# The end of a decoder trunk on one core: the last accumulation in two column groups, its squares in three parts, its update in three pieces

## The chip, the core and the metric

The kernel runs on one core of a Trainium2 chip, in one launch. The metric is the device time of an execution in microseconds. Five engines work side by side, each through its own queue of instructions: TensorE (PE, with its weight loads shown as PEld), VectorE (DVE), ScalarE (ACT), GpSimd (POOL) and SyncE (SP). SP, ACT and POOL also issue transfers.

## The reference

A decoder trunk of two layers on 256 tokens of 1024 columns in float32. The first layer mixes tokens by a gated linear recurrence, the second by attention with a forget gate. In each layer a half-step feed-forward block stands before and after the mixer. What matters here is the very last step, the second feed-forward block of the second layer:

```python
def rms_norm(x, g):
    xf = x.astype(jnp.float32)
    y = xf * lax.rsqrt(jnp.mean(xf * xf, axis=-1, keepdims=True) + EPS)
    return (y * g.astype(jnp.float32)).astype(x.dtype)

def swiglu(x, w_gate, w_up, w_down):
    return (jax.nn.silu(x @ w_gate) * (x @ w_up)) @ w_down
...
        f = swiglu(rms_norm(h, ffn2_pre_g[layer]), ffn2_w_gate[layer], ffn2_w_up[layer], ffn2_w_down[layer])
        h = h + 0.5 * rms_norm(f, ffn2_post_g[layer])
    return h
```

`w_down` is 2816 x 1024. The last norm needs the sum of squares over all 1024 columns of a token before any column of the output can be finished.

## The kernel before, in words

The 256 tokens are two halves of 128 (t = 0 and t = 1), which lie on the 128 partitions. `h[0]` and `h[1]` hold the residual stream, 128 x 1024 each. Every matrix is worked through in items of up to 1024 columns of weights: an item is loaded into a `raw` tile, split into an upper and a lower part (`whi` by ACT, `wlo` by DVE), and multiplied with both halves of the tokens. A product of full precision is made of three on TensorE (`mm3`): upper by upper, upper by lower part of the weights, lower part of the tokens by upper part of the weights. The input of the last matrix is the hidden layer, in `hhi` and `hlo`.

The order of TensorE's instructions is that in which the program is written (a manual schedule); the other engines' instructions are placed by a scheduler, with those under `tc.high_priority()` ahead. Half 0 leads and half 1 follows some items behind.

The last matrix `w_down` has 22 items of 128 rows (`row_items`). Each half has two accumulators of 128 x 512 in PSUM, `acc[t][0]` and `acc[t][1]`, of four `mm` tiles in all. For the last feed-forward block the last four items are kept for half 1 (`rows` = 4): they are first all multiplied into the first accumulator and then all into the second, so that the first is complete 12 products of 512 columns before the second:

```python
                    todo = [(kk, uu, n) for n in range(2) for (kk, uu) in kept[t]]
```

Then `post(t, acc[t])` calls `enter`, here with `last=True`. It does these steps for the half:

- `square_sum` on ACT, one for each accumulator: the squares go to a `junk` tile that nobody reads, their sum into a column of `ss`. One `junk` tile serves all.
- `rstd_of`: sum of the two columns plus epsilon (on DVE, tile `nv`), then the power -1/2 on POOL (`rstd`).
- the multiply of each accumulator by the gain `gb` on DVE, into a tile `t1` (512 columns each).
- `scalar_tensor_tensor` on DVE in pieces: `h` = `t1` times `rstd` plus `h`, and a transfer to `out` behind each piece. Half 0 has pieces of 256, 256 and 512 columns, all on SP's queue; half 1 has four of 256, on SP's and ACT's queues in turn.

In the profile the pages' names leave buffer numbers out; `mm_8053` and `mm_8054` in the rows of the order are the two accumulators of half 1, `mm_7982` and `mm_7983` those of half 0, `h_72` and `h_73` the halves of the stream.

Of the kernel before, what the change touches and what calls it, by code (L numbers as in the profile page):

```python
# [9 lines left out]
F32 = mybir.dt.float32  # L10
# [3 lines left out]
ALU = mybir.AluOpType  # L14
AX = mybir.AxisListType

P = 128
D = 1024
# [9 lines left out]
EPS = 1e-6  # L28
# [16 lines left out]
def trunk_kernel(ctx: ExitStack, tc: tile.TileContext, A: dict, out: bass.AP):  # L45
    nc = tc.nc
# [6 lines left out]
    spool = ctx.enter_context(tc.tile_pool(name="small", bufs=4))  # L53
# [4 lines left out]
    def nm(s):  # L58
        uid[0] += 1
        return f"{s}_{uid[0]}"  # L60

    def mmbank():
        return psum.tile([P, 512], F32, tag="mm", name=nm("mm"), bufs=4)

    def gtbank():
        return psum.tile([P, 512], F32, tag="gt", name=nm("gt"), bufs=2)
# [7 lines left out]
    def tensor_work(n):  # L74
        pace["t"] += n * 0.445e-3
# [5 lines left out]
    def defer(n, fn):  # L81
        pend.append([n, fn])
# [23 lines left out]
    h = [hpool.tile([P, D], F32, tag=f"h{t}", name=f"h{t}") for t in range(2)]  # L106
# [9 lines left out]
    mhalf = cpool.tile([P, 1], F32, name="mhalf")  # L116
# [48 lines left out]
    def split(rawv, parts, n, pieces=1, pin=False):  # L165
        u = Unit()
        hi = wpool.tile([P, 1024], F32R, tag="whi", name=nm("whi"), bufs=WB)
        lo = wpool.tile([P, 1024], F32R, tag="wlo", name=nm("wlo"), bufs=WB)
        m = n // pieces
        for c in range(0, n, m):  # L170
            up = nc.scalar.activation(hi[:parts, c:c + m], rawv[:, c:c + m], AF.Copy)  # L171
            if settled[0] or pin:
                tc.keep_in_program_order(up)
                settled[0] = False
            nc.vector.tensor_tensor(lo[:parts, c:c + m], rawv[:, c:c + m], hi[:parts, c:c + m].bitcast(F32), ALU.subtract)  # L175
        u.hi, u.lo = hi[:parts, :n], lo[:parts, :n]
        return u

    def mm3(ps, xh, xl, wh, wl, first, last):
        tensor_work(3 * wh.shape[1])  # L180
        nc.tensor.matmul(ps, xh, wh, start=first, stop=False)  # L181
        nc.tensor.matmul(ps, xh, wl, start=False, stop=False)  # L182
        nc.tensor.matmul(ps, xl, wh, start=False, stop=last)  # L183
# [9 lines left out]
    def rstd_of(ss, n, f=1.0, add=nc.gpsimd):  # L193

        v = spool.tile([P, 1], F32, tag="nv", name=nm("nv"))
        add.tensor_scalar(v, ss[:, 0:1], ss[:, 1:2] if n == 2 else 0.0, D * EPS * f * f, ALU.add, ALU.add)  # L196
        r = spool.tile([P, 1], F32, tag="rstd", name=nm("rstd"), bufs=8)
        nc.gpsimd.tensor_tensor(r, v, mhalf, ALU.pow)
        return r

    def square_sum(src, acc, f=1.0):
        junk = spool.tile([P, D], BF16, tag="junk", name=nm("junk"), bufs=1)
        nc.scalar.activation(junk[:, :src.shape[1]], src, AF.Square, scale=f, accum_out=acc)  # L203

    def new_ss():
        return spool.tile([P, 2], F32, tag="ss", name=nm("ss"))

    def to_tp(src, n):

        tp = gtbank()  # L210
        for j in range(4):
            nc.tensor.transpose(tp[:, j * P:(j + 1) * P], src[:, n * 512 + j * P:n * 512 + (j + 1) * P], ident)  # L212
        return tp
# [14 lines left out]
    def to_x(tps, dest):  # L228

        with tc.high_priority():  # L230
            xg = [x_upper(tps[n], dest, n) for n in range(2)]
            for n in range(2):
                x_lower(xg[n], dest, n)

    def to_x_tiles(tps, dest):

        gi, xh, xl = dest

        def operands(k):
            return tps[k // 4][:, k % 4 * P:(k % 4 + 1) * P], gT[:, gi + k:gi + k + 1]  # L240
        with tc.high_priority():
            for k in range(8):
                src, g = operands(k)
                nc.scalar.activation(xh[:, k, :], src, AF.Copy, scale=g)
            for k in range(8):
                src, g = operands(k)
                nc.vector.scalar_tensor_tensor(xl[:, k, :], src, g, xh[:, k, :].bitcast(F32), ALU.mult, ALU.subtract)
# [4 lines left out]
    def stat(t):  # L252
        ss = new_ss()
        square_sum(h[t], ss[:, 0:1])
        rs[t] = rstd_of(ss, 1)

    def enter(t, dests, pf, gb, half, last=False, normed=False, wait=3):

        f = 1.0 / 16 if half else 1.0 / 32
        ss = new_ss()  # L260
        t1 = []
        urgent = tc.high_priority()
        urgent.__enter__()
        for n in range(2):
            square_sum(pf[n], ss[:, n:n + 1], f)
        for n in range(2):
            if n == 1 and last:
                r = rstd_of(ss, 2, f, nc.vector)
            t1.append(hpool.tile([P, 512], F32, tag="t1", name=nm("t1"), bufs=2))
            nc.vector.tensor_tensor(t1[n], pf[n], gb[:, n * 512:(n + 1) * 512], ALU.mult)  # L270
        if not last:
            r = rstd_of(ss, 2, f)

        sp, aq = nc.sync, nc.scalar
        pieces = [(n * 512, 512, None) for n in range(2)]
        if last:
            pieces = ([(0, 256, sp), (256, 256, sp), (512, 512, sp)] if t == 0 else
                      [(0, 256, sp), (256, 256, aq), (512, 256, sp), (768, 256, aq)])
        for c, m, q in pieces:
            hn, tn = h[t][:, c:c + m], t1[c // 512][:, c % 512:c % 512 + m]  # L280
            nc.vector.scalar_tensor_tensor(hn, tn, r[:, 0:1], hn, ALU.mult, ALU.add)
            if last:
                q.dma_start(out[0, t * P:(t + 1) * P, c:c + m], hn)
        urgent.__exit__(None, None, None)
        if last:
            return

        def inputs():
            tps = [to_tp(h[t], n) for n in range(2)]
            for dest in dests:  # L290
                to_x(tps, dest)
            stat(t)

        def norm():
            with tc.high_priority():
                normed_x()

        def normed_x():
            ss = new_ss()
            for n in range(2):  # L300
                square_sum(h[t][:, n * 512:(n + 1) * 512], ss[:, n:n + 1])
            rs[t] = rstd_of(ss, 2)
            hn = []
            for n in range(2):
                hn.append(hpool.tile([P, 512], F32, tag="t1", name=nm("hn"), bufs=2))
                nc.vector.tensor_scalar(hn[n], h[t][:, n * 512:(n + 1) * 512], rs[t][:, 0:1], None, ALU.mult)

            def go():
                tps = []
                for n in range(2):  # L310
                    tp = gtbank()
                    for j in range(4):
                        nc.tensor.transpose(tp[:, j * P:(j + 1) * P], hn[n][:, j * P:(j + 1) * P], ident)
                    tps.append(tp)
                to_x_tiles(tps, dests[0])
            defer(6, go)

        if normed:
            norm()
            settled[0] = True  # L320
        else:
            defer(wait, inputs)
# [116 lines left out]
    def row_items(w, widths, get_x, post, rows=2, rows0=2, late=False):  # L439

        acc = {}
        kept = [[], []]
        nk = len(widths)
        r0 = 0
        for k, kp in enumerate(widths):
            def prep(kp=kp, r0=r0, k=k):
                return split(load_raw(w[r0:r0 + kp, :], kp, D), kp, D, pin=late and k > 3)

            def work(t, u, k=k):
                if k == 0:
                    acc[t] = [mmbank(), mmbank()]
                m = rows if t == 1 else rows0
                if k >= nk - m:
                    kept[t].append((k, u))
                    if k < nk - 1:
                        return
                    todo = [(kk, uu, n) for n in range(2) for (kk, uu) in kept[t]]
                else:  # L460
                    todo = [(k, u, n) for n in range(2)]
                for (kk, uu, n) in todo:
                    mm3(acc[t][n], *get_x(t, kk), uu.hi[:, n * 512:(n + 1) * 512], uu.lo[:, n * 512:(n + 1) * 512],
                        kk == 0, kk == nk - 1)
                if k == nk - 1:
                    post(t, acc[t])
            items.append((prep, work))
            r0 += kp
# [10 lines left out]
    def ffn_items(pool_of, wg, wu, wd, post_g, next_dests, last=False, normed=False):  # L479
# [52 lines left out]
        def post_down(t, accs):  # L532
            enter(t, next_dests(t), accs, box["gb"], True, last, normed)
# [47 lines left out]
    sp = rw.tile([RT, NRT], F32, name="sp")  # L581
# [738 lines left out]
```

## Time and profile before

| | us |
|---|---|
| median of 3 runs | 994.86 |
| lowest and highest run | 994.63, 995.75 |
| the profiled execution | 994.69 |
| its span | 993.0 |
| TensorE busy | 984.4 (99%) |
| VectorE busy | 618.5 (62%) |
| ScalarE busy | 530.5 (53%) |
| GpSimd busy | 47.0 (5%) |

The span is the time from the first to the last recorded instruction of one execution; the execution's own time also holds what lies around it. Busy shares are averages over stages. TensorE's ends are modelled, since products are pipelined: the step from one product's start to the next says more than the duration of one. The read of a sum on ACT (ACTIVATION_READ_ACCUMULATOR) stands behind each square and belongs to it.

### The profile page before, as it was taken

Reading aid. Unit: us, or ns where it says so; the run is one execution under the profiler, and the core shown is the slowest. Engines: PE = TensorE matmul, PEld = TensorE weight load, DVE = VectorE, ACT = ScalarE, POOL = GpSimd, SP = SyncE. Lnnn points to the kernel's source line nnn. Section 1 sums busy time; section 2 is a strip of 40 time slices with the busy share of each in tenths; the row PEclk is TensorE's granted clock in tenths of the full one; section 3 lists DMA queues with packets and bytes.
Section 4 is the critical chain, followed back from the end, with each engine's and each line's share of the span. In section 5 each row is a group of like instructions: output and inputs, shape, how many; then the busy total and the mean of one; then the engine's idle time right before and its main releaser. Section 6 shows DMA issues by size and latency. Waiting matters only on the chain.

```text
span 993.0 us, 12910 instructions
## 1 busy us (share of the span) xinstructions
PE 984.4 (99%) x4776; PEld 816.9 (82%) x4776; DVE 618.5 (62%) x792; ACT 530.5 (53%) x752; POOL 47.0 (5%) x92
## 2 busy tenths in 40 slices
PE   9999999999999999999999999999999999999997
PEld 6888888898988888888898888888888788888886
DVE  6756554668997555554686655554488876555542
ACT  7545443568886544443564444444366765444431
POOL 2400000100003000000100000000020000000000
PEclk9999999999999999999999999999999999999999
DMA  8967556465346766555567666655542467665531
GB/s 287 310 192 206 189 190 190 150 199 160 119 132 190 217 182 191 191 182 188 131 199 237 175 187 190 190 173 190 188 172 64 126 195 212 189 189 191 182 116 42
DMA packets 92645, 178.89 MB, mean 180 GB/s; under 512 B 11966, under 2 KB 32614, under 8 KB 92582
## 3 DMA queue, kind: packets, MB, share of 16 engines
q1 hardware_dynamic: 90998, 176.89, 58.0%
q10 hardware_dynamic: 752, 1.06, 0.3%
q8 instruction: 37, 0.61, 0.3%
q0 software_dynamic: 832, 0.12, 0.1%
q14 instruction: 26, 0.21, 0.1%
HBM read 176.95 MB, written 1.05 MB: 179 GB/s over the span
## 4 chain that ended last, share of the span: by engine, by line
PE 97%; issue 1%; DMA 1%; DVE 1%; ACT 0%; POOL 0%; POOLq 0%; DVEq 0%; ACTq 0%
PE mm L181 29%; PE mm L183 29%; PE mm L182 28%; PE tr L508 2%; PE gt L739 2%; PE gt L1040 1%; PE mm L188 1%; PE mm L190 1%; PE mm L189 1%; PE mm L1169 1%; PE mm L1075 1%; DMA raw<-in_ffn_w_gate_dram 1%; PE tr L1061 1%; PE gt L212 1%; PE tr L936 0%
## 5 line engine op out<-in xcount | busy, mean ns | idle before, releaser
L175 DVE TENSOR_TENSOR wlo<-raw,whi 128x1024 fp32r<-128x1024 f32 (+4 forms) x329 | 395.7, 1208 | 271.5 <-ACT whi L171 270.9
L171 ACT ACTIVATE whi<-raw 128x1024 fp32r<-128x1024 f32 (+4 forms) x329 | 341.8, 1045 | 317.1 <-PE mm L183 253.8
L181 PE MATMUL mm<-whi,xhi 128*128 128x512 f32 (+2 forms) x768 | 303.7, 395 | 0.0
L183 PE MATMUL mm<-whi,xlo 128*128 128x512 f32 (+2 forms) x768 | 298.9, 389 | 0.3 <-DVE xlo L226 0.3
L182 PE MATMUL mm<-wlo,xhi 128*128 128x512 f32 (+2 forms) x768 | 298.1, 388 | 0.0
L183 PEld LDWEIGHTS mm<-whi,xlo 128*128 128x128 f32 x768 | 144.2, 188 | 31.0 <-DVE xlo L226 0.7
L181 PEld LDWEIGHTS mm<-whi,xhi 128*128 128x128 f32 x768 | 144.3, 188 | 28.7 <-issue 1.3
L182 PEld LDWEIGHTS mm<-wlo,xhi 128*128 128x128 f32 x768 | 144.5, 188 | 27.9 <-DVE wlo L175 0.3
L181 PE MATMUL mm<-whi,hhi 128*128 128x512 f32 x352 | 138.2, 393 | 0.0
L183 PE MATMUL mm<-whi,hlo 128*128 128x512 f32 x352 | 138.0, 392 | 0.0
L182 PE MATMUL mm<-wlo,hhi 128*128 128x512 f32 x352 | 137.5, 391 | 0.0
L182 PEld LDWEIGHTS mm<-wlo,hhi 128*128 128x128 f32 x352 | 66.1, 188 | 14.3
L183 PEld LDWEIGHTS mm<-whi,hlo 128*128 128x128 f32 x352 | 66.1, 188 | 14.0
L181 PEld LDWEIGHTS mm<-whi,hhi 128*128 128x128 f32 x352 | 66.1, 188 | 13.8
L502 DVE SCALAR_TENSOR_TENSOR prod<-mm,rstd,sil 128x512 f32<-128x512 f32 (+1 forms) x48 | 33.9, 706 | 37.7 <-PE mm L183 34.0
L493 ACT ACTIVATE sil<-mm,rstd 128x512 f32<-128x512 f32 (+1 forms) x48 | 31.2, 652 | 40.6 <-PE mm L183 40.5
L196 POOL TENSOR_SCALAR nv<-ss 128x1 f32<-128x1 f32 x22 | 9.5, 432 | 722.2 <-ACT junk L203 722.2
L512 ACT ACTIVATE hhi<-tr 128x512 fp32r<-128x512 f32 (+1 forms) x48 | 26.6, 554 | 15.4 <-PE tr L508 15.3
L203 ACT ACTIVATE junk<-mm 128x512 bf16<-128x512 f32 x24 | 14.3, 597 | 32.9 <-PE mm L183 32.8
L270 DVE TENSOR_TENSOR t<-mm,gb 128x512 f32<-128x512 f32 x24 | 16.2, 689 | 24.9 <-ACT junk L203 24.8
L513 DVE TENSOR_TENSOR hlo<-tr,hhi 128x512 fp32r<-128x512 f32 (+1 forms) x48 | 30.5, 643 | 1.4
L181 PE MATMUL mm<-whi,zhi 128*128 128x340 f32 (+2 forms) x80 | 28.3, 354 | 0.0
(195 smaller groups left out, 898.0 us busy)
## 6 DMA issues: line engine op xcount, KB each, us to landing
raw<-in_ffn_w_down_dram SPq DMA_DIRECT2D x88, 512.0 KB
raw<-in_ffn_w_up_dram SPq DMA_DIRECT2D x80, 512.0 KB
raw<-in_ffn_w_gate_dram SPq DMA_DIRECT2D x78, 512.0 KB
raw<-in_rg_w_in_dram SPq DMA_DIRECT2D x20, 504.0 KB
raw<-in_rg_w_out_dram SPq DMA_DIRECT2D x10, 504.0 KB
raw<-in_ffn_w_gate_dram SPq DMA_DIRECT2D x18, 256.0 KB
raw<-in_ffn_w_up_dram SPq DMA_DIRECT2D x16, 256.0 KB
raw<-in_w_kv_dram SPq DMA_DIRECT2D x8, 512.0 KB
```

The costliest lines, as they stand in the source:

```text
L171: up = nc.scalar.activation(hi[:parts, c:c + m], rawv[:, c:c + m], AF.Copy)
L175: nc.vector.tensor_tensor(lo[:parts, c:c + m], rawv[:, c:c + m], hi[:parts, c:c + m].bitcast(F32), ALU.subtract)
L181: nc.tensor.matmul(ps, xh, wh, start=first, stop=False)
L182: nc.tensor.matmul(ps, xh, wl, start=False, stop=False)
L183: nc.tensor.matmul(ps, xl, wh, start=False, stop=last)
L270: nc.vector.tensor_tensor(t1[n], pf[n], gb[:, n * 512:(n + 1) * 512], ALU.mult)
L493: nc.scalar.activation(s[:, :nn], ps, AF.Silu, scale=rs[t][:, 0:1])
L502: nc.vector.scalar_tensor_tensor(pr[:, :nn], ps, rs[t][:, 0:1], s, ALU.mult, ALU.mult)
L508: nc.tensor.transpose(tp[:, j * P:(j + 1) * P], pr[:, j * P:(j + 1) * P], ident)
L512: nc.scalar.activation(hv, tp[:, :nn], AF.Copy)
L513: nc.vector.tensor_tensor(lv, tp[:, :nn], hv.bitcast(F32), ALU.subtract)
L739: nc.tensor.matmul(ps[j][:w, g * S:(g + 1) * S], wv[rows, o:o + w], xc[rows, k, :], start=start, stop=stop, skip_group_check=True)
```

## The change

Four things, all at the end of the program:

- In the last item of `w_down`, for half 1, the last two of the kept items are multiplied into the second accumulator in two column groups of 256: first both items for columns 512 to 767, then both for 768 to 1023.
- For half 1 a new function `finish` replaces the steps of `enter`. It squares the first accumulator (512 columns) and then the two column groups (256 each), into three columns of one tile `ss_end`; adds the first two with epsilon and then the third on DVE; multiplies by the gain in place, into `gb`.
- It updates `h[1]` in three pieces of 384, 384 and 256 columns, whose transfers go to SP, ACT and SP.
- For half 0 the pieces are four of 256, all on SP.

```diff
+    def finish(pf, gb, f):
+
+        ss = spool.tile([P, 4], F32, name="ss_end", bufs=1)
+        r = spool.tile([P, 1], F32, tag="rstd", name=nm("rstd"), bufs=8)
+        with tc.high_priority():
+            for i, (c, m) in enumerate([(0, 512), (512, 256), (768, 256)]):
+                src = pf[c // 512][:, c % 512:c % 512 + m]
+                square_sum(src, ss[:, i:i + 1], f)
+                if i == 1:
+                    nc.vector.tensor_scalar(ss[:, 3:4], ss[:, 0:1], ss[:, 1:2], D * EPS * f * f, ALU.add, ALU.add)
+                elif i == 2:
+                    nc.vector.tensor_scalar(ss[:, 3:4], ss[:, 2:3], ss[:, 3:4], 0.0, ALU.add, ALU.add)
+                    nc.gpsimd.tensor_tensor(r, ss[:, 3:4], mhalf, ALU.pow)
+                if i != 1:
+                    n = i // 2 * 512
+                    nc.vector.tensor_tensor(gb[:, n:n + 512], pf[i // 2], gb[:, n:n + 512], ALU.mult)
+            for c, m, q in ((0, 384, nc.sync), (384, 384, nc.scalar), (768, 256, nc.sync)):
+                hn = h[1][:, c:c + m]
+                nc.vector.scalar_tensor_tensor(hn, gb[:, c:c + m], r[:, 0:1], hn, ALU.mult, ALU.add)
+                q.dma_start(out[0, P:, c:c + m], hn)
+
     def enter(t, dests, pf, gb, half, last=False, normed=False, wait=3):
 
         f = 1.0 / 16 if half else 1.0 / 32
+        if last and t == 1:
+            return finish(pf, gb, f)
...
-        sp, aq = nc.sync, nc.scalar
+        sp = nc.sync
         pieces = [(n * 512, 512, None) for n in range(2)]
         if last:
-            pieces = ([(0, 256, sp), (256, 256, sp), (512, 512, sp)] if t == 0 else
-                      [(0, 256, sp), (256, 256, aq), (512, 256, sp), (768, 256, aq)])
+            pieces = [(c, 256, sp) for c in range(0, D, 256)]
...
-                for (kk, uu, n) in todo:
-                    mm3(acc[t][n], *get_x(t, kk), uu.hi[:, n * 512:(n + 1) * 512], uu.lo[:, n * 512:(n + 1) * 512],
-                        kk == 0, kk == nk - 1)
+                todo = [(kk, uu, n * 512, 512) for (kk, uu, n) in todo]
+                if k == nk - 1 and t == 1 and m == 4:
+                    todo[-2:] = [(kk, uu, c, 256) for c in (512, 768) for (kk, uu, _, _) in todo[-2:]]
+                for (kk, uu, c, w_) in todo:
+                    mm3(acc[t][c // 512][:, c % 512:c % 512 + w_], *get_x(t, kk), uu.hi[:, c:c + w_], uu.lo[:, c:c + w_],
+                        kk == 0, kk == nk - 1 and (w_ == 512 or c == 768))
```

On TensorE the end of its order changes so; `mm_8054` is the second accumulator of half 1, `whi_8266` and `whi_8284` are the upper parts of the last two items. First the rows before:

```order
L181 MATMUL mm_8054<-whi_8266,hhi_7264 128x512
L182 MATMUL mm_8054<-wlo_8267,hhi_7264 128x512
L183 MATMUL mm_8054<-whi_8266,hlo_7265 128x512
L181 MATMUL mm_8054<-whi_8284,hhi_7264 128x512
L182 MATMUL mm_8054<-wlo_8285,hhi_7264 128x512
L183 MATMUL mm_8054<-whi_8284,hlo_7265 128x512
```

and now, where the first six are those of columns 512 to 767 and the last six those of columns 768 to 1023:

```order
L181 MATMUL mm_8054<-whi_8266,hhi_7264 128x256
L182 MATMUL mm_8054<-wlo_8267,hhi_7264 128x256
L183 MATMUL mm_8054<-whi_8266,hlo_7265 128x256
L181 MATMUL mm_8054<-whi_8284,hhi_7264 128x256
L182 MATMUL mm_8054<-wlo_8285,hhi_7264 128x256
L183 MATMUL mm_8054<-whi_8284,hlo_7265 128x256
L181 MATMUL mm_8054<-whi_8266,hhi_7264 128x256
L182 MATMUL mm_8054<-wlo_8267,hhi_7264 128x256
L183 MATMUL mm_8054<-whi_8266,hlo_7265 128x256
L181 MATMUL mm_8054<-whi_8284,hhi_7264 128x256
L182 MATMUL mm_8054<-wlo_8285,hhi_7264 128x256
L183 MATMUL mm_8054<-whi_8284,hlo_7265 128x256
```

Six products of 512 columns have become twelve of 256, and nothing ahead of them has moved. On ScalarE, the end of the order with the semaphores that each instruction waits for (- before, + now); the squares of half 0 stand in the first two rows:

```order
 L203 ACTIVATE junk_8349,ss_8348<-mm_7982 128x512 [waits PE_49]
 L203 ACTIVATE junk_8351,ss_8348<-mm_7983 128x512 [waits PE_49,Activation_49]
-L203 ACTIVATE junk_8398,ss_8397<-mm_8053 128x512 [waits PE_49,Activation_49]
-L203 ACTIVATE junk_8400,ss_8397<-mm_8054 128x512 [waits PE_49,Activation_49]
-L283 DMA out_dram<-h_73 128x256 [waits DVE_49] x2
+L203 ACTIVATE junk_8407,ss_end<-mm_8053 128x512 [waits PE_49,Activation_49]
+L203 ACTIVATE junk_8410,ss_end<-mm_8054 128x256 [waits PE_49,Activation_49]
+L203 ACTIVATE junk_8413,ss_end<-mm_8054 128x256 [waits Activation_49]
+L276 DMA out_dram<-h_73 128x384 [waits DVE_49]
```

Of half 1's second square two have become, of which the later one has a wait for ACT itself alone, and one transfer has left ACT's queue. On DVE, the end of the order now, from half 1's first multiply on:

```order
L272 TENSOR_TENSOR gb_7430<-mm_8053,gb_7430 128x512 [waits Activation_49]
L266 TENSOR_SCALAR ss_end<-ss_end 128x1 [waits Activation_49]
L268 TENSOR_SCALAR ss_end<-ss_end 128x1 [waits DVE_49,Activation_49]
L272 TENSOR_TENSOR gb_7430<-mm_8054,gb_7430 128x512 [waits PE_49]
L275 SCALAR_TENSOR_TENSOR h_73<-gb_7430,rstd_8406,h_73 128x384 [waits Pool_49]
L275 SCALAR_TENSOR_TENSOR h_73<-gb_7430,rstd_8406,h_73 128x384 [waits DVE_49]
L275 SCALAR_TENSOR_TENSOR h_73<-gb_7430,rstd_8406,h_73 128x256
```

The second multiply stands behind both adds, as it stood behind the one before.

## The prediction

> **What bounds the kernel now.** I read the page first: its busy shares and its chain of waits. Then the timeline of the last 15 us, since the edit touches nothing before them, and for prices the rows of instructions grouped by shape.
>
> ```profile
> PE 984.4 (99%) x4776; PEld 816.9 (82%) x4776; DVE 618.5 (62%) x792; ACT 530.5 (53%) x752; POOL 47.0 (5%) x92
> PE 97%; issue 1%; DMA 1%; DVE 1%; ACT 0%; POOL 0%; POOLq 0%; DVEq 0%; ACTq 0%
> ```
>
> TensorE is busy for 99% of the span and makes 97% of the chain. The span (993.0 us) is that of one profiled execution whose time was 994.69 us, so 1.69 us lie around it; the median of the three runs shown is 994.86 us, 0.17 us above. I make every sum as a difference against the profiled execution and add it to the median.
>
> TensorE's last product ends near 986.87, and the span runs on to 993.0: a tail of 6.13 us, in which TensorE does nothing. This is the tail, from the timeline (start, duration, engine, line, operation):
>
> ```profile
> 985.33 0.39 PE L181 MATMUL mm<-whi,hhi 128*128 128x512 f32 x1
> 986.47 0.40 PE L183 MATMUL mm<-whi,hlo 128*128 128x512 f32 x1
> 986.97 0.60 ACT L203 ACTIVATE junk<-mm 128x512 bf16<-128x512 f32 x1 [2.06 <-PE mm L183]
> 987.46 0.19 ACT L203 ACTIVATION_READ_ACCUMULATOR junk<-mm 128x1 f32 x1
> 987.69 0.21 DVE L196 TENSOR_SCALAR nv<-ss 128x1 f32<-128x1 f32 x1 [2.06 <-ACT junk L203]
> 987.82 0.68 DVE L270 TENSOR_TENSOR t<-mm,gb 128x512 f32<-128x512 f32 x1
> 987.98 0.55 POOL L198 TENSOR_TENSOR rstd<-nv,mhalf 128x1 f32<-128x1 f32 x1 [6.32 <-DVE nv L196]
> 988.56 1.67 DVE L281 SCALAR_TENSOR_TENSOR h<-t,rstd,h 128x256 f32<-128x256 f32 x4
> 989.08 0.33 SPq L283 DMA_DIRECT2D out_dram<-h  x1
> 990.27 0.35 ACTq L283 DMA_DIRECT2D out_dram<-h  x1
> ```
>
> It is one chain: last product, square of the second half and its sum (ACT), sum plus epsilon (DVE), power -1/2 (POOL), four updates of 256 columns (DVE), each with its transfer. The multiply by the gain (987.82 to 988.50) lies beside the power (987.98 to 988.53) and ends 0.03 us before it. Behind the updates come the bytes, in windows of time (us of length, busy time of the engines, clock, DMA share, GB/s):
>
> ```profile
> 988.50:989.90 1.40, 0.00 (x0) 0.00 (x0) 1.34 (x4) 0.00 (x0) 0.03 (x1) 1.00 0.00 0
> 989.90:991.70 1.80, 0.00 (x0) 0.00 (x0) 0.34 (x1) 0.00 (x0) 0.00 (x0) 0.66 0.87 291
> 991.60:991.70 0.10, 0.00 (x0) 0.00 (x0) 0.00 (x0) 0.00 (x0) 0.00 (x0) 0.50 0.05 10
> 991.70:993.00 1.30, 0.00 (x0) 0.00 (x0) 0.00 (x0) 0.00 (x0) 0.00 (x0) 0.50 0.00 0
> ```
>
> The first bytes move at 989.90, 0.82 us after the first issue (989.08). 291 GB/s for 1.80 us is 524 KB, the whole second half of the output. The share is 0.87, so without pauses the rate would be 334 GB/s, and 524 KB would take 1.57 us. The last bytes move near 991.65; the 1.35 us behind them I carry over unchanged.
>
> So at most a few tenths of the 6.13 us are at stake. 0.2% is 2.0 us, about what a measurement of this kernel can tell from no change.
>
> **The change part by part.**
>
> *The products in two column groups.* Six products of 512 columns become twelve of 256. From the two PE rows above, five steps take 1.14 us: 0.228 us a product. For 256 columns there are rows elsewhere in this kernel, the recurrent block's input projection; here the first and the last of 33 in a row, and their group:
>
> ```profile
> 229.81 0.28 PE L188 MATMUL mm<-xhi,whi 128*126 128x256 f32 x1
> 233.57 0.28 PE L190 MATMUL mm<-xhi,wlo 128*126 128x256 f32 x1
> L188 PEld LDWEIGHTS mm<-xhi,whi 128*126 128x126 f32 x80 | 14.9, 186 | 0.2
> L183 PEld LDWEIGHTS mm<-whi,hlo 128*128 128x128 f32 x352 | 66.1, 188 | 14.0
> ```
>
> 3.76 us over 32 steps is 0.1175 us a product, with a weight load of 186 ns for each: the loads overlap, or the pace would be 0.186. The loads at the end are of the same size (188 ns), so I take 0.1175. The twelfth product starts at 985.33 + 11 x 0.1175 = 986.62 and ends 0.28 later, at 986.90, against 986.87: **+0.03 us**. Bounds: at half of 0.228 a product the end is 986.86 (-0.01); at one per weight load, 0.188, it is 985.33 + 11 x 0.188 + 0.28 = 987.68 (+0.81, a rival below). [...]
>
> *The squares in three parts.* The gain would be a square of columns 512 to 767 that runs while TensorE still multiplies columns 768 to 1023. The order of ScalarE's instructions denies it. The second square waits for PE, and the third, which reads the columns that the very last product writes, carries no wait for PE at all. Its cover can only be the wait of the second square before it on the same engine, so that one is already for the last product. Both column groups lie in the one tile of 128x512. [...]
>
> So two squares of 256 stand behind the last product where one of 512 stood. For the price of a short one I have these groups (mean ns of one behind the bar):
>
> ```profile
> L493 ACT ACTIVATE sil<-mm,rstd 128x512 f32<-128x512 f32 x40 | 27.4, 688 | 32.7 <-PE mm L183 32.7
> L493 ACT ACTIVATE sil<-mm,rstd 128x256 f32<-128x256 f32 x8 | 3.8, 475 | 7.9 <-PE mm L183 7.9
> ```
>
> 256 columns fewer save 0.213 us. The square of 512 hands over to the reading of its sum after 0.49 us (986.97 to 987.46); one of 256 does so after 0.28. Then 0.19 for the reading. Between two squares stands a wait of the engine for itself (both write the same junk tile). These two places show such a step:
>
> ```profile
> 186.58 0.18 ACT L203 ACTIVATION_READ_ACCUMULATOR junk<-h 128x1 f32 x1
> 186.80 0.63 ACT L203 ACTIVATE junk<-h 128x512 bf16<-128x512 f32 x1
> 775.05 0.47 ACT L1048 ACTIVATE pe<-gt,mx 128x256 f32<-128x256 f32 x1
> 775.42 0.19 ACT L1048 ACTIVATION_READ_ACCUMULATOR pe<-gt,mx 128x1 f32 x1
> 775.52 0.46 ACT L1048 ACTIVATE pe<-gt,mx 128x256 f32<-128x256 f32 x1
> ```
>
> With that wait the next one starts 0.04 us after the reading's end (186.76 to 186.80); without it, 0.10 us after the reading's start (775.42 to 775.52). I take the first, because the order shows that wait. Second square: 987.00 to its reading's end at 987.47. Third: 987.51, reading 987.79 to 987.98. The add on DVE starts 0.04 later, at 988.02, against 987.69: **+0.33 us**, with the +0.03 in it. Bounds: without the wait, 0.38 between the squares, it is +0.20; with 0.37 per square as at 775.05 (an exponential with a bias, from the same memory), +0.51. A gain is excluded here, as the last square cannot start sooner and one more stands ahead of it.
>
> The sum is now two adds on DVE. The first needs only the second square and lies at 987.51 to 987.72, under the third square; cover gone, it would cost its 0.21. The second takes the place of the old one (0.21). From there to the update nothing differs: multiply and power start and end as late after the add as before. Update starts at 988.56 + 0.33 = 988.89.
>
> *The update in three pieces.*
>
> ```profile
> L281 DVE SCALAR_TENSOR_TENSOR h<-t,rstd,h 128x512 f32<-128x512 f32 x21 | 14.9, 750 | 2.4 <-POOL rstd L198 2.4
> L281 DVE SCALAR_TENSOR_TENSOR h<-t,rstd,h 128x256 f32<-128x256 f32 x6 | 2.6, 480 | 0.1
> 981.70 1.55 DVE L281 SCALAR_TENSOR_TENSOR h<-t,rstd,h 128x256 f32<-128x256 f32 x3
> 984.60:984.80 0.20, 0.20 (x2) 0.16 (x2) 0.00 (x0) 0.20 (x2) 0.00 (x0) 1.00 1.00 379
> ```
>
> One of 256 takes 0.48, one of 512 0.75, so one of 384 takes 0.615 (halfway). Four of 256 took 1.67, so each follows the one before after 0.40, and one of 384 after 0.53. The three end at 988.89 + 2 x 0.53 + 0.48 = 990.43, against 990.23. A transfer is issued 0.04 after its piece. First issue: 988.89 + 0.615 + 0.04 = 989.55 (before 989.08, **+0.47**). Last issue: 990.47 (before 990.27, **+0.20**). SP is free for it: its first issue is over at 989.88. ScalarE issues the middle one at 990.07 and has nothing else.
>
> *The bytes.* First bytes at 989.55 + 0.82 = 990.37; 1.57 us of transfer without a pause end at 991.94, against 991.65: **+0.29 us**. That is later than the last issue allows (+0.20), so I take +0.29. Bounds: rows of 1.5 KB may move faster than those of 1 KB; the 2 KB rows of the first half's last piece went at 379 GB/s (row above), 1.38 us, and then the last issue rules, +0.20.
>
> *The first half's output in four.* The update of 512 becomes two of 256: four take 1.67 where three took 1.55, so DVE ends near 983.4, and its next work came at 984.94. SP issues four transfers of 0.33 and its next issue is at 989.55; some of them wait for the semaphores of earlier weight loads, whose rows TensorE has multiplied by then. Cost: nothing, covered by 5 us of TensorE's products; bare it would be 0.12 us.
>
> The multiply now writes into the gain's own tile: same shape, same 0.68.
>
> **Sum:** 0.03 for PE and 0.30 for ACT put the update 0.33 later, the larger pieces let the bytes begin 0.47 later, and the bytes flow without a pause and give 0.18 back: +0.29. Profiled execution 994.69 + 0.3 = 995.0; median 994.86 + 0.3 = **995.2 us**. With the bounds together: +0.1 to +0.5.
>
> **The rivals.**
>
> *The column groups are released apart* (the change does what its split suggests). First group's end: 985.33 + 5 x 0.1175 + 0.28 = 986.20. Its square runs at 986.30 and is over by 986.77; the last square, at 987.00, by 987.47; add at 987.51, 0.18 sooner than before; update at 988.38, first issue 989.04, bytes from 989.86 to 991.43: -0.22 us, 994.6 us. For it: 256 columns end 0.7 us before the rest. Against: the third square's row has no wait for PE.
>
> *The weight loads set the pace of the short products*, 0.188 each: PE +0.81, the rest +0.26: +1.07, 995.9 us. For it: load 188 ns, longer than the product's step. Against: the 33 products at 0.1175 with loads of 186.
>
> *The short products don't overlap their loads at all*, the one way to a slower kernel that can be told. At 0.28 + 0.188 = 0.468 a product the last one ends at 985.33 + 11 x 0.468 + 0.28 = 990.76: PE +3.89, in all +4.15, 999.0 us. It passes 0.2% once PE ends 1.73 later, from 0.272 us a product on. For it: two groups now go into one tile in turn, for which the profile has no row. Against: the same 33 products.
>
> **How the numbers follow.** Forecast 0.75, released apart 0.10, pace of the loads 0.07, no overlap 0.05, and 0.03 for a gain over 0.2% that I see no way to. Forecast, first and second rival are all within 0.2% (992.9 to 996.8): same 0.92, slower 0.05, faster 0.03. The range: the three runs shown reach 0.23 below and 0.89 above their median. Down: the first rival less 0.23, 994.4. Up: the forecast plus 0.89, 996.1, which also takes in the second rival. About 0.1 to 0.15 is left out.
>
> **What would show it.** Right: the last twelve products 0.12 apart; both squares of 256 behind the last product, 0.5 apart; the last add at 1.1 us after the last product's end instead of 0.8; first issue near 2.65 us behind it, bytes without a pause. A square that starts before the last product ends makes the first rival true; steps of 0.19 or more between products the second or third; a difference before the last 15 us would make the whole reading wrong.

## The result, and the profile after

| | us |
|---|---|
| before, median of 6 runs | 994.94 |
| changed kernel, median of 6 runs | 1001.05 |
| lowest and highest of these | 1000.83, 1002.18 |
| the profiled execution, its span | 1002.0, 1000.3 |

The ratio is 1.0064, with a 95% interval of 1.0054 to 1.0075: 6.1 us slower, where +0.3 had been forecast. The profiled execution is one of the two slowest of the six, about 1 us above their median.

The page of the changed kernel, busy time and chain:

```profile
PE 991.9 (99%) x4782; PEld 818.5 (82%) x4782; DVE 618.6 (62%) x793; ACT 531.3 (53%) x754; POOL 46.9 (5%) x92
PE 97%; issue 1%; DVE 1%; DMA 0%; POOL 0%; ACT 0%; POOLq 0%; DVEq 0%; SPq 0%; ACTq 0%
```

All other engines are busy as long as before, to within 0.8 us (ScalarE); TensorE 7.5 us longer, with six products more. The tail, from the timeline and from windows of time, as the prediction showed it of before:

```profile
992.31 0.28 PE L181 MATMUL mm<-whi,hhi 128*128 128x256 f32 x1
...
993.59 0.28 PE L183 MATMUL mm<-whi,hlo 128*128 128x256 f32 x1
...
993.96 0.38 ACT L203 ACTIVATE junk<-mm 128x256 bf16<-128x256 f32 x1 [2.11 <-PE mm L183]
994.25 0.19 ACT L203 ACTIVATION_READ_ACCUMULATOR junk<-mm 128x1 f32 x1
994.47 0.38 ACT L203 ACTIVATE junk<-mm 128x256 bf16<-128x256 f32 x1
...
994.98 0.21 DVE L268 TENSOR_SCALAR ss_end<-ss_end 128x1 f32<-128x1 f32 x1 [0.29 <-ACT junk L203]
...
995.85 1.54 DVE L275 SCALAR_TENSOR_TENSOR h<-gb,rstd,h 128x384 f32<-128x384 f32 x3
996.50 1.26 SPq L276 DMA_DIRECT2D out_dram<-h  x2
...
997.30:999.00 1.70, 0.00 (x0) 0.00 (x0) 0.10 (x1) 0.00 (x0) 0.00 (x0) 0.50 0.88 309
999.00:1000.30 1.30, 0.00 (x0) 0.00 (x0) 0.00 (x0) 0.00 (x0) 0.00 (x0) 0.50 0.00 0
```

TensorE ends at 993.87, 7.0 us later than before (986.87). From there on the tail takes 6.43 us, where it took 6.13. So 0.3 us are in the tail and the rest lies ahead of it, where the order of the instructions had not changed at all. The steps between products show it. Here are products of the down projections, two that lie 36 steps apart without a pause between them, in the first feed-forward block (near 151 us) and in the last (near 951), of before:

```profile
150.97 0.39 PE L183 MATMUL mm<-whi,hlo 128*128 128x512 f32 x1
...
159.13 0.39 PE L183 MATMUL mm<-whi,hlo 128*128 128x512 f32 x1
...
950.77 0.39 PE L183 MATMUL mm<-whi,hlo 128*128 128x512 f32 x1
...
959.01 0.39 PE L183 MATMUL mm<-whi,hlo 128*128 128x512 f32 x1
```

and of the changed kernel:

```profile
151.24 0.40 PE L183 MATMUL mm<-whi,hlo 128*128 128x512 f32 x1
...
159.64 0.40 PE L183 MATMUL mm<-whi,hlo 128*128 128x512 f32 x1
...
950.77 0.40 PE L183 MATMUL mm<-whi,hlo 128*128 128x512 f32 x1
...
959.17 0.40 PE L183 MATMUL mm<-whi,hlo 128*128 128x512 f32 x1
```

36 steps took 8.16 us (226.7 ns each) in the first block and 8.24 (228.9) in the last; they take 8.40 (233.3) in both now. The products on `xhi` and `xlo` have not changed: 12 steps take 2.72 us (226.7 ns each) before and after.

```profile
850.17 0.39 PE L183 MATMUL mm<-whi,xlo 128*128 128x512 f32 x1
...
852.89 0.40 PE L183 MATMUL mm<-whi,xlo 128*128 128x512 f32 x1
```

```profile
851.28 0.39 PE L183 MATMUL mm<-whi,xlo 128*128 128x512 f32 x1
...
854.00 0.39 PE L183 MATMUL mm<-whi,xlo 128*128 128x512 f32 x1
```

Every product here has two operands in the on-chip memory: one is loaded into TensorE first (the trace's LDWEIGHTS rows, 128 x 128, 0.19 us each), the other is streamed past it (the MATMUL rows, 512 columns of `whi` or `wlo`). The two kinds of product differ in where their loaded operand lies. The built program's list of tiles gives it, in bytes within a partition and, behind the slash, within 256 bytes:

```
                                 before          after
whi, wlo (streamed)              38304 / 160     38304 / 160
xhi                              120224 / 160    120224 / 160
ss_end                           -               147616 (takes 32 bytes)
hhi, first block, half 0         177824 / 160    177856 / 192
hhi, other blocks, half 0        179040 / 96     179072 / 128
```

`ss_end` is the one tile that the change adds. It ends the pool of small tiles, and everything that is allocated behind that pool moved on by 32 bytes: `hhi`, `hlo` and, under the same tags, `zhi` and `zlo`; `y`, `oh` and `ol`. `whi`, `wlo`, `xhi` and `xlo` lie ahead of it. With the steps above, 264 products of the first block cost 6.6 ns more each and 792 of the others 4.4: 1.7 + 3.5 = 5.2 us. Another 324 products on `y`, `zhi` and `oh` had moved too; by their steps in the two traces (227.5 ns before and 233.3 now for 52 steps in a row on `y`, of which there are 132; 228.7 and 233.0 for 40 on `zhi`, 229.1 and 233.2 for 22 on `oh`) they cost some 1.4 us more, an estimate at 6 ns for those on `y` and 3 to 4 for the others. Together that is about 6.6 us of the 7.0 by which TensorE ended later in these two executions.

### The profile page after: what moved, and what is told of

The parts are those of the page before. It is cut to its first block, busy times and chain, and to the rows that moved or that the text cites. A ratio compares the mean times of both kernels' runs of the same rounds, so it can differ in the third digit from the quotient of the medians.

```text
span 1000.3 us, 12927 instructions
## 1 busy us (share of the span) xinstructions
PE 991.9 (99%) x4782; PEld 818.5 (82%) x4782; DVE 618.6 (62%) x793; ACT 531.3 (53%) x754; POOL 46.9 (5%) x92
## 4 chain that ended last, share of the span: by engine, by line
PE 97%; issue 1%; DVE 1%; DMA 0%; POOL 0%; ACT 0%; POOLq 0%; DVEq 0%; SPq 0%; ACTq 0%
PE mm L181 29%; PE mm L183 28%; PE mm L182 28%; PE tr L533 2%; PE gt L764 2%; PE mm L1194 1%; PE gt L1065 1%; PE mm L188 1%; PE mm L190 1%; PE mm L189 1%; PE mm L1100 1%; PE tr L1086 1%; PE gt L212 1%; DMA raw<-in_ffn_w_gate_dram 0%; PE tr L961 0%
## 5 line engine op out<-in xcount | busy, mean ns | idle before, releaser
L181 PE MATMUL mm<-whi,hhi 128*128 128x512 f32 x354 | 140.4, 397 | 0.0
L203 ACT ACTIVATE junk<-mm 128x512 bf16<-128x512 f32 (+1 forms) x25 | 14.5, 580 | 33.5 <-PE mm L183 33.4
```

## The experiments

Two theories stood against each other at first: *address* (the 32 bytes cost the 6 us) and *change* (what the edit does costs them).

**32 bytes alone.** The kernel before, with an unused tile:

```diff
+    spool.tile([P, 8], F32, name="pad", bufs=1)
     psum = ctx.enter_context(...)
```

> The kernel before, with one unused tile of 32 bytes a partition in the pool of small tiles, and nothing else. Everything allocated behind that pool, hhi and hlo among it, then lies 32 bytes further on, as in the changed kernel. Theory 'address' (the new tile ss_end moved hhi, hlo, y, zhi and oh by 32 bytes, and every product of 512 columns that loads its weights from them takes some 4.5 ns more: 1362 of them, 6.1 us): about 1001.0 us, with steps of 233 ns between products on hhi and 227 on xhi. Theory 'change' (the products in column groups, the squares or the transfers cost the 6 us): no change, 994.9 us.

Measured: 1000.60 us against 994.93, ratio 1.0057 (1.0045 to 1.0070). Two products 36 steps apart near 951 us (lines are one further on here):

```profile
950.84 0.39 PE L183 MATMUL mm<-wlo,hhi 128*128 128x512 f32 x1
...
959.24 0.39 PE L183 MATMUL mm<-wlo,hhi 128*128 128x512 f32 x1
```

8.40 us for 36 steps: the changed kernel's step, without its change. *Address* stands, and *change* is out as the source of more than a few tenths.

**The shift made 128 bytes.**

```diff
-        ss = spool.tile([P, 4], F32, name="ss_end", bufs=1)
+        ss = spool.tile([P, 32], F32, name="ss_end", bufs=1)
```

> The changed kernel with ss_end made 128 bytes a partition instead of 16 (it took 32), so that everything behind it lies 128 bytes further on than in the kernel before and has the same place within 128 bytes as there. Theory 'address': the 6 us are gone, what is left is the tail, +0.3 us: 995.2 us, and hhi is back at 227 to 230 ns a step. Theory 'change': 1001.0 us.

Measured: 1000.97 us, ratio 1.0059 (1.0047 to 1.0072). A miss: I had taken the period for 64 or 128 bytes. The steps near 151 and 951 us:

```profile
151.21 0.40 PE L183 MATMUL mm<-whi,hlo 128*128 128x512 f32 x1
...
159.58 0.40 PE L183 MATMUL mm<-whi,hlo 128*128 128x512 f32 x1
...
951.22 0.40 PE L183 MATMUL mm<-whi,hlo 128*128 128x512 f32 x1
...
959.62 0.40 PE L183 MATMUL mm<-whi,hlo 128*128 128x512 f32 x1
```

8.37 us (232.5 ns) and 8.40 (233.3). If a place repeats, then at more than 128 bytes.

**Both operands moved, and the streamed one alone.** First 32 bytes ahead of everything:

```diff
+    cpool.tile([P, 8], F32, name="pad")
     wpool = ctx.enter_context(...)
```

> The kernel before with an unused tile of 32 bytes in the very first pool, so that both operands of the products move by 32 bytes: the weights that stream (whi, wlo) and the ones that are loaded (xhi, hhi and the rest). Theory 'difference' (what counts is the distance of the two operands' addresses within 64 bytes): no change, 994.9 us. Theory 'place' (what counts is the place of the loaded operand alone: at a multiple of 64 bytes it is slow): all 3700 products of 512 columns slow, 227 to 229 ns become 233, +21 us, 1015 us.

Measured: 995.01 us, ratio 0.9999 (0.9990 to 1.0008). Then the same, with 96 bytes more behind `whi` and `wlo`:

```diff
+    cpool.tile([P, 8], F32, name="pad")
     wpool = ctx.enter_context(...)
...
+    hpool.tile([P, 24], F32, name="pad2")
     h = [hpool.tile(...
```

> The kernel before with 32 bytes unused in the first pool and 96 more behind whi and wlo: the operand that streams (whi, wlo) moves by 32 bytes, the loaded ones (xhi, hhi and the rest) by 128, so that they keep their place within 128 bytes. Theory 'difference': every product has its operands 32 bytes apart within 64, 233 ns a step also on xhi, +21 us, 1015 us. Theory 'place': no change, 994.9 us.

Measured: 1014.80 us, ratio 1.0198 (1.0184 to 1.0212). Products on `xhi` and `xlo` of the kernel before, 12 steps apart, and of this one (lines two further on), 15 steps apart:

```profile
850.17 0.39 PE L183 MATMUL mm<-whi,xlo 128*128 128x512 f32 x1
...
852.89 0.40 PE L183 MATMUL mm<-whi,xlo 128*128 128x512 f32 x1
```

```profile
849.92 0.40 PE L185 MATMUL mm<-whi,xlo 128*128 128x512 f32 x1
...
853.43 0.40 PE L185 MATMUL mm<-whi,xlo 128*128 128x512 f32 x1
```

226.7 ns became 234.0. In these runs it is the distance of the two operands that counts, not the place of either: moved together by 32 bytes they lose nothing (995.01 us against 994.93), moved apart the products on `xhi` and `xlo` lose 7.3 ns a step as well, and the kernel 19.9 us. (The loaded operands moved by 128 bytes here, which was meant to leave their places as they were. By the run with the shift of 128 bytes it does not, so the distances are 96 bytes for `xhi` and the first block and 32 for the others, and not 32 throughout; *place* is refuted by the run with 32 bytes ahead of everything alone, 995.01 us.)

**A shift of 256 bytes, and none.**

```diff
-        ss = spool.tile([P, 4], F32, name="ss_end", bufs=1)
+        ss = spool.tile([P, 64], F32, name="ss_end", bufs=1)
```

> The changed kernel with ss_end made 256 bytes a partition; everything behind it moves by 256 bytes (128 bytes left all 6 us in place). Theory 'within 256': 995.2 us, steps of 227 ns in the first block and 229 in the others. Theory 'farther' (the period is more than 256 bytes, or any move of these tiles costs): 1001 us.

Measured: 995.30 us against 994.82, ratio 1.0004 (0.9995 to 1.0014). And with `ss_end` in a buffer that exists:

```diff
-        ss = spool.tile([P, 4], F32, name="ss_end", bufs=1)
+        ss = spool.tile([P, 4], F32, tag="mx", name="ss_end")
```

> The changed kernel with ss_end in a buffer of a tag that is there already (mx, the same size), so that nothing moves. Every theory of addresses: the tail alone, +0.3 us, 995.2 us, steps on hhi as in the kernel before. Theory 'change': 1001.0 us.

Measured: 995.21 us, ratio 1.0006 (0.9997 to 1.0015). Both as expected. The steps are back, with 256 bytes near 951 us 8.24 for 36:

```profile
951.02 0.39 PE L183 MATMUL mm<-whi,hlo 128*128 128x512 f32 x1
...
959.26 0.39 PE L183 MATMUL mm<-whi,hlo 128*128 128x512 f32 x1
```

So the change itself costs 0.4 us, not told apart from nothing by these runs, and 256 bytes give the same as none (995.30 and 995.21 us).

**Other distances.** Unused bytes at the head of the feed-forward pools (192, 224 and 192):

```diff
         pools[key] = cm.__enter__()
+        pad = {"ffn_a": 48, "ffn_b": 56, "ffn_c": 48}.get(name)
+        if pad:
+            pools[key].tile([P, pad], F32, name=f"pad_{name}")
```

> The kernel before with unused bytes at the head of the feed-forward pools, so that hhi and hlo lie at other distances from whi and wlo within 256 bytes: -64 in the first block (was 0), -96 in the second and third (was -64), 128 in the last (was -64). Theory 'within 256': 229 ns a step in the first block, 232 to 234 in the others, 994.9 + 0.5 + 2.5 + 0.9 = 998.8 us. Rival 'block' (the first block is faster for a reason of its own, not its place): 227 there still.

Measured: 998.98 us, one run. The first block, now at -64, has the step that the others had before; the second, at -96, one near those of 32 and 64; and the last, at 128, that of the first in the run with 128 bytes:

```profile
151.12 0.39 PE L183 MATMUL mm<-whi,hlo 128*128 128x512 f32 x1
...
159.36 0.39 PE L183 MATMUL mm<-whi,hlo 128*128 128x512 f32 x1
...
455.28 0.40 PE L183 MATMUL mm<-whi,hlo 128*128 128x512 f32 x1
...
463.68 0.40 PE L183 MATMUL mm<-whi,hlo 128*128 128x512 f32 x1
...
951.02 0.40 PE L183 MATMUL mm<-whi,hlo 128*128 128x512 f32 x1
...
959.39 0.40 PE L183 MATMUL mm<-whi,hlo 128*128 128x512 f32 x1
```

8.24 (228.9 ns), 8.40 (233.3) and 8.37 (232.5). The first block was not faster for a reason of its own.

**The good distance for all.**

```diff
+        lp.tile([P, 16], F32, name="pad")
         kv["kT"] = lp.tile([HA, NH, S], F32, name="kT")
```

> The kernel before with 64 unused bytes in the pool of keys and values, so that hhi, hlo, zhi and oh of the last three feed-forward blocks and of the attention lie 64 bytes further on: at the same place within 256 bytes as whi and wlo, where those of the first block lie already (their steps were 227 ns, those of the others 229). Theory 'within 256' (the two operands' distance within 256 bytes sets the step: 0 gives 227 ns, -64 gives 229, all others seen 232 to 234): 984 products of 512 columns gain some 2 ns, 2 us: 993 us. Theory 'within 64' (only 32 bytes or none counts): no change, 994.9 us.

Measured: 993.05 us against 994.82, ratio 0.9983 (0.9974 to 0.9992): faster than both kernels, by 64 bytes that nobody uses. Near 951 us the step is that of the first block, 8.16 for 36:

```profile
950.86 0.39 PE L183 MATMUL mm<-whi,hlo 128*128 128x512 f32 x1
...
959.02 0.39 PE L183 MATMUL mm<-whi,hlo 128*128 128x512 f32 x1
```

**A bank for the last column group.** Without the shift, columns 768 to 1023 accumulate for all 22 items in a tile of their own, and the multiply follows each square:

```diff
                     acc[t] = [mmbank(), mmbank()]
+                    if rows == 4 and t == 1:
+                        acc[t].append(gtbank())
...
+                    bank = acc[t][2] if apart and c == 768 else acc[t][c // 512]
```

> The changed kernel without the shift (as in e6_after_no_shift), with the columns 768 to 1023 of the last accumulation in a bank of their own, for all 22 items; the multiply by the gain follows in three parts. Now the second square reads a bank that no product writes any more. Theory 'bank' (the second square waits for the last product because both column groups lie in one bank): it starts some 0.6 us before the last product ends, the add follows 0.5 us sooner behind it (0.6 us instead of 1.1); 54 more splits of a product into two of 256 cost 54 x 4 ns = 0.2 us: 994.9 us. Rival 'order' (the squares stay behind the last product for another reason): 995.4 us, add at 1.1 us.

Measured: 994.62 us, ratio 0.9997 (0.9988 to 1.0006). The comparison by time says no more than "no different from before"; the trace does. The last product, the two squares and the last add, first where both groups share a bank (the run without the shift), then here:

```profile
987.86 0.28 PE L183 MATMUL mm<-whi,hlo 128*128 128x256 f32 x1
988.24 0.38 ACT L203 ACTIVATE junk<-mm 128x256 bf16<-128x256 f32 x1 [2.05 <-PE mm L183]
...
988.74 0.38 ACT L203 ACTIVATE junk<-mm 128x256 bf16<-128x256 f32 x1
...
989.25 0.21 DVE L268 TENSOR_SCALAR ss_end<-ss_end 128x1 f32<-128x1 f32 x1 [0.29 <-ACT junk L203]
```

```profile
986.95 0.28 PE L183 MATMUL gt<-whi,hlo 128*128 128x256 f32 x1
986.64 0.39 ACT L203 ACTIVATE junk<-mm 128x256 bf16<-128x256 f32 x1 [1.35 <-PE mm L183]
...
987.32 0.38 ACT L203 ACTIVATE junk<-gt 128x256 bf16<-128x256 f32 x1 [0.21 <-PE gt L183]
...
987.83 0.21 DVE L268 TENSOR_SCALAR ss_end<-ss_end 128x1 f32<-128x1 f32 x1
```

With a bank for each, the first of the two squares starts 0.59 us before the last product ends (986.64 against 987.23), and the add follows that end by 0.60 us instead of 1.11. So *order* is out, and the shared accumulator was what held the square back. The group has got a tile and a bank of its own at once here; which of the two the program's wait goes by is not told apart.

**Both gains.** The same with the 64 bytes:

```diff
+        lp.tile([P, 16], F32, name="pad")
         kv["kT"] = lp.tile([HA, NH, S], F32, name="kT")
```

> e8_own_bank with the 64 unused bytes of e3_before_kv64: every large operand that is loaded as weights lies at the same place within 256 bytes as the one that streams, and the last column group has a bank of its own. If the two are independent, the gains add: 993.05 - 0.2 = 992.9 us. Rival 'same' (the tail's gain is lost in the shorter steps): 993.1 us.

Measured: 993.88 us against 994.85, ratio 0.9990 (0.9981 to 0.9999). A miss of 1.0 us against the sum, and no better than the 64 bytes alone. The short products lost; 24 of them in a row (23 steps), without the 64 bytes and with them:

```profile
984.34 0.28 PE L181 MATMUL mm<-whi,hhi 128*128 128x256 f32 x1
...
986.95 0.28 PE L183 MATMUL gt<-whi,hlo 128*128 128x256 f32 x1
```

```profile
982.85 0.28 PE L181 MATMUL mm<-whi,hhi 128*128 128x256 f32 x1
...
985.60 0.28 PE L183 MATMUL gt<-whi,hlo 128*128 128x256 f32 x1
```

113.5 ns a step at a distance of -64, 119.6 at 0: of these two distances the products of 256 columns do better at the one where those of 512 do worse. At 6.1 ns each, 132 of them lose 0.8 us, which is most of the miss.

## Why the prediction was wrong

- **The step that failed** stands in the prediction's opening: "the edit touches nothing before them", the last 15 us. That holds for the order of the instructions, as does "nothing ahead of them has moved" in the section on the change. It does not hold for the addresses: from the first block on, products on tiles that had moved took some 3 to 7 ns longer each. The sum has no term for the new tile's bytes, and the prediction priced `ss_end` as two adds on DVE only. 32 bytes alone made 5.7 of the 6.1 us, and without the shift the change came to 995.21, which is the forecast. The prediction's own last sign against itself, "a difference before the last 15 us", is the one that came true.
- **No rival had it.** The three rivals were all of the last 12 products and the square behind them. The slower one (no overlap of loads and products, +4.15 us) was given for the wrong place; the twelve took 0.1164 us a step (1.28 us over 11), with 0.1175 forecast. That these agree so closely is in part luck: the price came from products at other addresses, and where nothing is shifted the same twelve take 0.113 (1.24 us over 11, in the run with `ss_end` in a buffer that exists).
- **What would have shown it.** The product's step was read from five steps in the last block alone, 0.228, and not compared between blocks. The same instruction took 226.7 ns in the first block and 228.9 in the last, at the same clock (1.00 granted in both stretches) and with nothing waited for. That difference was in the trace before; that addresses make it was shown only by the run with other distances (228.9 ns in the first block too, once its operands lay at -64). That a new tile moves what lies behind it stands in the two programs' lists of tiles.
- **The tail was right**, from TensorE's end on, forecast and then measured in the changed kernel: last add +1.12 and +1.11; update +1.99 and +1.98; first issue +2.65 and +2.63. First bytes to last took 1.57 us in the forecast and some 1.6 in the trace (997.3 to 998.95). The tail grew by 0.26 us in the forecast and by 0.30 in the trace. Here the agreement is step by step, not by luck of the sum.
- **The shared accumulator.** That the column groups in one accumulator would not be released apart was read from the waits in ScalarE's order, and the trace has it so: in the changed kernel the last product ends at 993.87 and the first of the two squares starts at 993.96. In the run where each group has a bank of its own it started 0.59 us before the last product's end. Why the wait is set as it is was not shown.
- **The range** (994.4 to 996.1) took the forecast, the first rival and the scatter of three runs. It had nothing for products slower everywhere, so it could not hold 1001.

## What to carry to other kernels

A new tile can move every address behind it, however few bytes it takes (16 asked for and 32 taken here; 32 alone cost 5.7 us): compare the two programs' lists of tiles before calling an edit local, and give a small scratch tile a buffer that exists (995.21 us here instead of 1001.05). In a kernel bound by TensorE, compare the steps of the same product between stages; where they differ with nothing waited for (226.7 and 228.9 ns here), look at where the operands lie. Splitting an accumulation into column groups let the reader start early here only when each group had a tile and bank of its own: 0.59 us before the last product's end, against 0.10 after it with one for both (988.24 against 988.14).

## What the runs showed of the hardware

In these runs the step of a product of 128 x 512 (the operands' type is float32r, `F32R` in the kernel) went with the distance between the loaded operand's and the streamed operand's addresses within a partition. Loaded minus streamed, in bytes within 256:

| distance | ns a step, 512 columns | read from | ns a step, 256 columns | read from |
|---|---|---|---|---|
| 0 | 226.7 | before, near 151 and 851 us; e3, near 951 | 119.6 | e9 |
| -64 | 228.9 | before and e7, near 951 us; e10, near 151 | 113.5 | e8 |
| 32, -32 | 233.3 | after, near 151 (32) and 951 us (-32); e1, near 951 (-32) | 116.4 (at -32) | after |
| 64 | 233.3 | e2, near 951 us | | |
| 96 | 234.0 | e5, near 851 us | | |
| -96 | 233.3 | e10, near 459 us | | |
| 128 | 232.5 | e2, near 151 us; e10, near 951 | | |

Shifts of 32 and 128 bytes cost 6 us (1001.05 and 1000.97 us, against 994.94 and 994.93), one of 256 nothing beside the tail (995.30), and moving both operands together nothing (995.01). -64 and 64 are not alike (228.9 and 233.3 ns). The figures for 256 columns are of one stretch of one run each, of 11 to 23 steps. The granted clock was 0.998 to 1.000 in all these runs. So the step differed by up to 7.3 ns in 226.7 with how the two operands lie to each other. What inside TensorE or the memory makes the difference was not shown, nor why the products of 256 columns took less at -64 than at 0.
